# High parts of 32 attention-stage inputs: VectorE maximum over an axis of length one in place of a copy

## The chip, the cores and the metric

The kernel runs on one core of one Trainium2 chip. The metric is device microseconds (us) of one launch; the time before is the median of three runs. Engines are named as in the profile: PE is TensorE's matmul, PEld its weight load, DVE is VectorE, ACT ScalarE, POOL GpSimd, SP SyncE.

## The reference

One hybrid decoder layer in float32 on a sequence of 2048 rows of width 1024. Cut to what matters here:

```python
proj = h @ w_in[l]
x_rnn, z_rnn, q, k, v, z_attn, g_r, g_a = jnp.split(proj, IN_SPLITS, axis=-1)
...
y_rnn = (hr * jax.nn.silu(z_rnn)) @ w_out_rnn[l]             # RG-LRU branch, projected
...
o = dilated_attention_mixture(qh, kh, vh).reshape(B, S, D_ATTN)   # 8 heads of 128, three (window, dilation) groups
y_attn = (o * jax.nn.silu(z_attn)) @ w_out_attn[l]           # attention branch, projected
merged = jax.nn.sigmoid(g_r + bg_r) * y_rnn + jax.nn.sigmoid(g_a + bg_a) * y_attn
x = x + gate[:, None, :] * (merged @ w_o[l])
```

## The kernel before, in words

Every matmul operand is split into a high part, rounded to the PE's float32r type, and a low part, the difference; a product is three matmuls, high by high, high by low and low by high (`mm3`, line 152). So each operand costs one rounding copy and one subtraction on some engine. The helpers are `hi_act` (line 160, ScalarE), `hi_dve` (line 163, a VectorE copy, CAST in the profile), `lo_pool` (line 166, a GpSimd subtraction) and `lo_dve` (line 169, a VectorE subtraction).

The launch has three stages that follow one another: the input projection with the recurrence (to about 1340 us), attention (about 1340 to 1870 us), and the rest of the output projections with the last product.

Attention runs over 16 heads-and-halves of six units each. All engines follow one order written out by hand (`tc.manual_schedule`): each slot makes the scores of one unit (tiles `sc`), its exponentials (`pp`), and, seven slots later, the scaled and transposed weights (`pT`, split into `pth` and `ptl`) and the sums `o`. The transposes of line 1562 go to PSUM tiles `pT` that come free when the `ptl` subtraction has read them. GpSimd makes the low parts `kq`, `vh`, `wh` of the loaded keys, queries and values, and copies queries into window order (`q`, line 1436), which the window scores read. Once for each head-and-half, the softmax weights `M` are made by a chain of small VectorE instructions, lines 1648 to 1674, and ScalarE scales `pp` with them (line 1542).

The gaps between the attention matmuls are filled with steps of other work, the generator `steps(jobs)`: the two output projections, products `pj` of 128x128 weights `S` by 128x512 inputs `yh` and `yl`. There are eight jobs `j`, each of 512 columns; the first four read the recurrence's output, the last four the attention's. A job's eight inputs `k` are loaded into a ring of raw tiles `R` and split by `split_y`, in steps that the table `SPLIT_Y` fixes, around the start of the job. Jobs 1 to 4 have their high parts made by VectorE: 4 jobs of 8 inputs, 32 copies. Their low parts come from GpSimd for even `k` and from VectorE, right behind the copy, for odd `k`. The products are evicted at line 1786 into `fg`.

## Time and profile before

| What | Value |
|---|---|
| time, median of 3 runs | 2168.0 us (2166.8 to 2169.54) |
| the profiled execution's own time | 2169.62 us |
| its span, first to last instruction | 2167.8 us |
| mean granted TensorE clock | 0.998 |
| busy share of the span: PE, DVE, ACT, POOL | 99%, 69%, 60%, 51% |

The span is the profiler's, 1.8 us shorter than that execution's time; the profiled execution is 1.6 us above the median. Busy shares are means over the launch, and a busy PE includes matmuls that are pipelined behind one another.

### The profile page before, as it was taken

How to read it: one execution, taken by the hardware profiler on the slowest of the kernel's cores; microseconds unless marked ns; L12 is line 12 of the kernel's file. 1: busy time of each engine (PE TensorE's matmuls, PEld its weight loads, DVE VectorE, ACT ScalarE, POOL GpSimd, SP SyncE). 2: the span in 40 equal slices, each digit the busy share in tenths (PEclk: the TensorE clock that was granted, in tenths of full speed). 3: DMA queues.
4: the chain of work that ended last, by engine and by line, in shares of the span. 5: the costliest groups of instructions: out<-in, count | busy, mean ns of one | idle time of the engine just before them, and what ended most of it. 6: DMA issues, size and time to landing. Idle time of an engine off the chain costs nothing.

```text
span 2167.8 us, 32585 instructions
## 1 busy us (share of the span) xinstructions
PE 2138.3 (99%) x10539; PEld 1787.8 (82%) x10539; DVE 1488.1 (69%) x2606; ACT 1296.9 (60%) x2591; POOL 1111.2 (51%) x868
## 2 busy tenths in 40 slices
PE   9999999999999999999999999999999999999998
PEld 6888778888888888888888887888888988878886
DVE  6759878768656725544536584687777787788887
ACT  5748668668644527457548532677878877444333
POOL 1467667777666323223234564466666564422444
PEclk9999999999999999999999999999999999999999
DMA  8467887886655378898996666988887777899553
GB/s 302 144 208 259 277 290 264 285 296 237 175 112 165 108 250 281 295 312 299 323 327 220 163 163 198 288 266 266 269 267 230 242 241 223 298 316 295 183 171 111
DMA packets 416431, 521.39 MB, mean 241 GB/s; under 512 B 107558, under 2 KB 282882, under 8 KB 415236
## 3 DMA queue, kind: packets, MB, share of 16 engines
q1 hardware_dynamic: 376244, 401.65, 59.7%
q10 hardware_dynamic: 34384, 99.78, 12.1%
q0 software_dynamic: 5632, 17.88, 2.6%
q8 instruction: 83, 1.36, 0.3%
q14 instruction: 88, 0.72, 0.1%
HBM read 332.02 MB, written 187.17 MB: 240 GB/s over the span
## 4 chain that ended last, share of the span: by engine, by line
PE 63%; DVE 5%; DMA 5%; POOL 3%; issue 3%; ACT 1%; SPq 1%; POOLq 0%; ACTq 0%; DVEq 0%
PE X L152 13%; PE V L152 13%; PE pj L152 8%; PE Z L152 7%; PE W L152 6%; PE Y L152 6%; PE sc L152 3%; PE o L152 3%; PE pg L152 1%; DMA fg<-mrT 1%; PE pT L1562 1%; POOL kq L166 1%; PE pT L1575 1%; DMA fg<-gaT 1%; DMA oT<-zt 1%
## 5 line engine op out<-in xcount | busy, mean ns | idle before, releaser
L166 POOL TENSOR_TENSOR S<-R,S 128x512 fp32r<-128x512 f32 x192 | 294.3, 1541 | 170.0 <-ACT S L160 87.3
L152 PE MATMUL V<-T,S 128*128 128x512 f32 x1344 | 324.2, 390 | 2.3 <-DVE ev L455 2.3
L152 PE MATMUL X<-T,S 128*128 128x512 f32 x1344 | 323.8, 390 | 1.5 <-ACT u L385 1.3
L152 PE MATMUL pj<-yh,S 128*128 128x512 f32 x896 | 322.1, 403 | 1.3 <-DVE fg L1786 0.8
L152 PEld LDWEIGHTS V<-T,S 128*128 128x128 f32 x1344 | 251.8, 188 | 56.3 <-issue 2.1
L152 PEld LDWEIGHTS X<-T,S 128*128 128x128 f32 x1344 | 251.7, 188 | 56.4 <-ACT u L385 3.0
L166 POOL TENSOR_TENSOR S<-s,S 128x512 fp32r<-128x512 f32 x116 | 170.6, 1471 | 151.1 <-ACT S L160 114.9
L152 PEld LDWEIGHTS pj<-yh,S 128*128 128x128 f32 x896 | 168.5, 188 | 32.6 <-DVE S L169 1.6
L1475 ACT ACTIVATE pp<-pp,st 128x256 f32<-128x256 f32 (+3 forms) x256 | 133.7, 523 | 73.1 <-DVE st L1474 71.7
L152 PE MATMUL pj<-yl,S 128*128 128x512 f32 x448 | 175.9, 393 | 0.6 <-POOL yl L166 0.3
L160 ACT ACTIVATE S<-s 128x512 fp32r<-128x512 f32 x124 | 77.4, 624 | 145.4 <-DVE s L285 91.0
L152 PE MATMUL W<-T,S 128*128 128x512 f32 x672 | 161.6, 389 | 0.0
L152 PE MATMUL Y<-T,S 128*128 128x512 f32 x672 | 161.5, 389 | 0.0
L152 PE MATMUL Z<-T,S 128*128 128x512 f32 x672 | 161.4, 389 | 0.0
L160 ACT ACTIVATE S<-R 128x512 fp32r<-128x512 f32 x200 | 121.6, 623 | 59.0 <-DMA R<-in_w_in_dram 14.8
L169 DVE TENSOR_TENSOR ptl<-pT,pth 128x384 fp32r<-128x384 f32 (+1 forms) x160 | 97.9, 628 | 76.0 <-ACT pth L160 73.7
L152 PEld LDWEIGHTS W<-T,S 128*128 128x128 f32 x672 | 126.0, 188 | 26.9 <-issue 0.9
L152 PEld LDWEIGHTS Z<-T,S 128*128 128x128 f32 x672 | 126.1, 188 | 26.2
L152 PEld LDWEIGHTS Y<-T,S 128*128 128x128 f32 x672 | 126.1, 188 | 26.1
L974 DVE SCALAR_TENSOR_TENSOR xc<-xr,par,xc 128x512 f32<-128x512 f32 x96 | 104.4, 1087 | 58.1 <-ACT xc L968 55.9
L166 POOL TENSOR_TENSOR s<-R,s 128x512 fp32r<-128x512 f32 x32 | 43.2, 1351 | 189.5 <-ACT s L160 173.0
L1542 ACT ACTIVATE pp<-pp,M 128x256 f32<-128x256 f32 (+3 forms) x256 | 117.9, 522 | 22.3 <-DVE M L1674 22.3
(417 smaller groups left out, 4922.8 us busy)
## 6 DMA issues: line engine op xcount, KB each, us to landing
sD<-S ACTq DMA_DIRECT2D x140, 512.0 KB, 3.8
S<-sD SPq DMA_DIRECT2D x140, 512.0 KB, 5.2
S<-wD SPq DMA_DIRECT2D x82, 512.0 KB, 5.6
R<-in_w_in_dram SPq DMA_DIRECT2D x144, 256.0 KB, 3.4
wD<-s ACTq DMA_DIRECT2D x64, 256.0 KB, 5.3
kraw<-kqT SPq DMA_DIRECT2D x32, 384.0 KB, 5.4
T<-in_w_mod_dram SPq DMA_DIRECT2D x16, 512.0 KB, 9.1
vN<-ev SPq DMA_DIRECT2D x32, 256.0 KB, 2.7
```

Source lines behind the costliest of these rows:

```text
L152: nc.tensor.matmul(o, lhsT=l, rhs=r, start=st, stop=sp, **kw)
L160: nc.scalar.activation(o, i, AF.Copy)
L166: nc.gpsimd.tensor_tensor(o, i, h.bitcast(F32), ALU.subtract)
L169: return nc.vector.tensor_tensor(o, i, h.bitcast(F32), ALU.subtract).ins
L974: nc.vector.scalar_tensor_tensor(xc, xr[:, i : i + CH], cw(i), xc, ALU.mult, ALU.add)
L1475: nc.scalar.activation(pdst, pdst, AF.Exp, bias=m_, scale=-1.0, accum_out=l_)
L1542: nc.scalar.activation(pp, pp, AF.Copy, scale=w)
L1562: nc.tensor.transpose(pt[:, c0 + j * P : c0 + (j + 1) * P], pp[i][:, k * P : (k + 1) * P], ident)
L1575: nc.tensor.transpose(pt[:, c * P : (c + 1) * P], pp[:, half * P : (half + 1) * P], ident)
```

## The change

`split_y` no longer calls the copy for jobs 1 to 4. It has VectorE take the maximum over an added innermost axis of length one, with the same tile read and the same tile written; a maximum of one number is that number, rounded on writing as the copy's was. The order of the instructions, what each waits for and every other instruction are as before, on all engines: on VectorE 32 rows of CAST become rows of TENSOR_REDUCE in the same places.

```diff
-                (hi_dve if 0 < j < NB + 1 else hi_act)(yh[:], t[:])
+                if 0 < j < NB + 1:
+                    nc.vector.tensor_reduce(yh[:], t[:].unsqueeze(2), AX.X, ALU.max)
+                else:
+                    hi_act(yh[:], t[:])
                 (lo_dve if (k % 2 if j else k > 4) or j > NB + 1 else lo_pool)(yl[:], t[:], yh[:])
```

## The prediction

> **What bounds the kernel now.** I read the page's engine shares first, then the busy time by stretches of the attention stage, then the PE's waits in it, and last the instructions in order of time around those waits.

> ```profile
> PE 2138.3 (99%) x10539; PEld 1787.8 (82%) x10539; DVE 1488.1 (69%) x2606; ACT 1296.9 (60%) x2591; POOL 1111.2 (51%) x868
> ```

> The PE is the bound: only 2167.8 - 2138.3 = 29.5 us of the span lack a matmul. Next come the stretches of the stage that holds the 32 copies (start:end, length, then busy time of PE, PEld, DVE, ACT, POOL).

> ```profile
> 1380.00:1620.00 240.00, 239.30 (x1578) 214.17 (x1578) 184.88 (x567) 191.34 (x587) 153.35 (x145) 1.00 0.86 272
> 1620.00:1640.00 20.00, 16.10 (x100) 13.22 (x99) 17.64 (x46) 10.80 (x27) 13.98 (x12) 1.00 0.65 191
> 1640.00:1760.00 120.00, 120.00 (x796) 109.23 (x795) 90.06 (x244) 103.29 (x260) 76.02 (x60) 1.00 0.79 244
> 1760.00:1780.00 20.00, 17.78 (x109) 15.88 (x107) 17.42 (x42) 14.64 (x40) 13.91 (x13) 0.91 0.66 194
> ```

> From 1380 to 1780 us the PE lacks 0.70 + 3.90 + 0 + 2.22 = 6.8 us. Nearly all of it lies in two stretches of 20 us. That is the most a cheaper high part can give back, unless waits hide inside matmuls. Who ended the PE's waits from 1380 to 1880 us (total us, times, longest):

> ```profile
> PE sc L152 <- POOL q L1436: 4.6, 5, 1.7
> PE pT L1562 <- DVE ptl L169: 1.3, 2, 0.7
> PE pT L1562 <- ACT pp L1542: 1.0, 2, 0.7
> PE pj L152 <- POOL yl L166: 0.3, 1, 0.3
> ```

> **The change: 32 copies go, 32 maxima come.** The groups of this stage, the first with min/median/max in ns, the others with busy us and mean ns:

> ```profile
> L163 DVE CAST yh<-R x32: 409/423/2073, 1394.5 to 1768.5; 128x512 fp32r<-128x512 f32 x32
> ...
> L163 DVE CAST yh<-R 128x512 fp32r<-128x512 f32 x32 | 22.6, 710 | 0.0
> ...
> L169 DVE TENSOR_TENSOR yl<-R,yh 128x512 fp32r<-128x512 f32 x18 | 19.7, 1101 | 0.5
> ```

> A copy that nothing holds up takes 0.42 us; the mean is 0.71. So 22.6 - 32 x 0.423 = 9.1 us are waiting inside the copies. The rows below say for what: each long copy spans a GpSimd instruction and ends just behind it.

> The trace has no 128x512 maximum. The nearest rows are VectorE's other reductions, and the pass of 512 numbers at line 1474:

> ```profile
> L1653 DVE TENSOR_REDUCE xs<-xq x16: 285/286/287, 1378.8 to 1837.9; 128x32 f32<-128x128 f32 x16
> ...
> L1658 DVE TENSOR_REDUCE sc<-xq x16: 215/217/220, 1379.0 to 1838.1; 128x16 f32<-128x64 f32 x16
> ...
> L1474 DVE CUSTOM_DVE_ANT_0 pp<-sc,msk 128x512 f32<-128x512 f32 x32 | 22.0, 689 | 1.1
> ```

> By numbers read, the slope is (286 - 217) / 64 = 1.08 ns, and 512 numbers cost 286 + 384 x 1.08 = 700 ns. By numbers written it is 69 / 16 = 4.3 ns, and 512 results cost 286 + 480 x 4.3 = 2350 ns: both reductions fold four numbers into one, so these rows can't tell the two apart. The lower end is the free copy's 423 ns. I take 0.69 us, since line 1474, which writes as many numbers as it reads, lies there too; 0.42 and 2.35 stay for the range.

> Does a maximum wait for GpSimd? Here a reduction runs inside a GpSimd instruction that lasts to 1632.58, and its 16 durations above differ by 2 ns. Line 1672, a small addition of two SBUF tiles, does wait when GpSimd is at work: 1.20 us there, 0.17 elsewhere.

> ```profile
> 1630.74 1.84 POOL L166 TENSOR_TENSOR kq<-kraw,kq 128x768 fp32r<-128x768 f32 x1
> ...
> 1631.15 0.29 DVE L1653 TENSOR_REDUCE xs<-xq 128x32 f32<-128x128 f32 x1
> ...
> 1634.71 1.29 POOL L166 TENSOR_TENSOR yl<-R,yh 128x512 fp32r<-128x512 f32 x1 [0.36 <-DVE yh L163]
> ...
> 1634.83 1.20 DVE L1672 TENSOR_TENSOR M<-M,t__3081_16175 128x16 f32<-128x16 f32 x1
> ...
> L1672 DVE TENSOR_TENSOR M<-M,t__3271_17104 x1: 174/174/174, 1701.7 to 1701.7; 128x16 f32<-128x16 f32 x1
> ```

> So the maximum does not wait. VectorE's total: 32 x 0.69 = 22.1 us against 22.6, next to nothing; what changes is where the time lies. A free copy gets 0.27 us longer, a held one up to 1.4 us shorter.

> [...]

> **Place one, 1615 to 1634 us.** Rows of the timeline (start, us):

> ```profile
> 1615.78 2.69 DVE L163 CAST yh<-R 128x512 fp32r<-128x512 f32 x2
> ...
> 1615.80 1.04 PE L1575 MATMUL pT<-cs,pp 128*128 128x128 f32 x8
> ...
> 1616.15 4.03 POOL L166 TENSOR_TENSOR kq<-kraw,kq 128x768 fp32r<-128x768 f32 x2
> ...
> 1618.51 2.22 DVE L169 TENSOR_TENSOR yl<-R,yh 128x512 fp32r<-128x512 f32 x1
> ...
> 1620.65 0.68 DVE L163 CAST pth<-pT 128x512 fp32r<-128x512 f32 x1
> ...
> 1622.20 0.63 PE L1562 MATMUL pT<-cs,pp 128*128 128x128 f32 x4 [0.65 <-DVE ptl L169]
> ...
> 1624.48 0.62 ACT L1475 ACTIVATE pp<-pp,st 128x384 f32<-128x384 f32 x1 [4.61 <-DVE st L1474]
> ...
> 1628.77 0.62 ACT L160 ACTIVATE vh<-vraw 128x512 fp32r<-128x512 f32 x1
> ...
> 1629.47 1.30 POOL L166 TENSOR_TENSOR vh<-vraw,vh 128x512 fp32r<-128x512 f32 x1 [2.70 <-DMA vraw<-vN]
> ...
> 1632.53 1.82 POOL L1436 CAST q<-kq 128x512 fp32r<-128x512 f32 x2
> ...
> 1633.39 0.51 PE L152 MATMUL sc<-kq,q 128*128 128x256 f32 x2 [1.05 <-POOL q L1436]
> ```

> Two copies sit out GpSimd's first `kq`; the subtraction behind them misses the gap and sits out the second. With maxima, VectorE reaches the subtraction at 1615.8 + 2 x 0.69 = 1617.2, before the first `kq` ends (about 1618.2, half of 4.03 on). It gets in there and ends at about 1618.8 instead of 1620.7. So `pth`, whose input the PE had made by 1616.8, starts 1.8 us earlier, and both PE waits on `ptl`, 1.3 us, go. Behind it ScalarE, which waited 4.61 us for VectorE, comes up to 1.8 us earlier too. Its `vh`, which ended at 1629.39, released GpSimd's `vh` (the transfer named there I read as landed before). From 1627.7 on, 1.30 for `vh`, 1.84 for `kq` and some 0.6 for the first `q` make 1631.4, where the PE got it at 1633.4. The PE asks for it 1.3 us earlier, so its wait of 1.05 shrinks to about 0.4. Gain here: 1.3 + 0.7 = 2.0 us. The price: GpSimd's second `kq` starts 0.5 us later, which its idle time before `vh` covers.

> **Place two, 1760 to 1772 us.**

> ```profile
> 1760.42 1.30 POOL L166 TENSOR_TENSOR vh<-vraw,vh 128x512 fp32r<-128x512 f32 x1
> 1760.52 1.49 DVE L163 CAST yh<-R 128x512 fp32r<-128x512 f32 x1
> ...
> 1761.69 2.03 POOL L166 TENSOR_TENSOR kq<-kraw,kq 128x768 fp32r<-128x768 f32 x1
> ...
> 1762.05 2.22 DVE L169 TENSOR_TENSOR yl<-R,yh 128x512 fp32r<-128x512 f32 x1
> ...
> 1764.19 1.14 DVE L169 TENSOR_TENSOR ptl<-pT,pth 128x512 fp32r<-128x512 f32 x2
> ...
> 1765.26 0.41 DVE L163 CAST yh<-R 128x512 fp32r<-128x512 f32 x1
> ...
> 1765.74 1.30 POOL L166 TENSOR_TENSOR yl<-R,yh 128x512 fp32r<-128x512 f32 x1 [2.02 <-DMA vraw<-vN]
> ...
> 1770.89 0.50 PE L152 MATMUL sc<-kq,q 128*128 128x256 f32 x2 [1.71 <-POOL q L1436]
> ```

> The maximum ends at 1761.2, the subtraction gets in when `vh` ends (1761.72) and ends at 1762.3 instead of 1764.3. The second high part, behind the two `ptl`, then ends near 1762.4 + 1.14 + 0.69 = 1764.2 instead of 1765.7, and GpSimd's `yl`, which I read as waiting for it and not for the transfer named, starts about 1.4 us earlier; `vh`, `kq` and `q` follow it. The PE lost 1.71 and then 0.52 us on these `q`; I take 1.3 us back, since a `yl` subtraction now gets in ahead of the first `q`.

> **Costs.** A maximum ahead of the chain that makes `M` delays it by up to 0.27 us, and behind it the PE waits for `pp` (1.0 us at present). For such chains in the later two rings of copies, 2 x 0.2 = 0.4 us. The other free copies have VectorE idle time behind them: 240.0 - 184.9 = 55 us from 1380 to 1620, where the PE lacks 0.7.

> **Sum.** 2.0 + 1.3 - 0.4 = 2.9 us. The profiled execution goes from 2169.6 to 2166.7, and as it was 1.6 us above the median, the median goes from 2168.0 to 2165.1.

> **The rivals.**

> *The wait only moves.* The subtraction behind the odd maxima reads two tiles of SBUF and waited as the copies did: 18 of them took 1.10 us in the mean, against 0.69. If it meets a GpSimd instruction each time, VectorE is no earlier at either place, and the time stays at 2168, with 0.4 us of cost 2168.4. For it: the 2.22 us rows. Against: in both rows the copy's own wait is what made it miss the gap. [...] Chance 0.27.

> *More comes back.* All 6.8 us of the PE's idle time, or the like with waits hidden in matmuls: 2161.2. For it: both places start from the same late VectorE. Against: `q` waits for three GpSimd instructions that the change leaves alone. Chance 0.22.

> *The maximum is paid by result, 2.35 us.* Slower than before: VectorE would have 32 x (2.35 - 0.71) = 52 us more. In the densest stretch

> ```profile
> 1400.00:1420.00 20.00, 19.88 (x137) 17.97 (x136) 17.51 (x56) 14.49 (x50) 14.37 (x15) 1.00 0.88 258
> ```

> six of a ring's eight copies add 9.8 us to 2.5 idle ones; 7.3 us on the path, four times, gives 2197. It decides once a maximum costs more than 0.71 + 2.5 / 6 = 1.1 us. Against: line 1474 writes 512 numbers in 0.69. Chance 0.06.

> *The change doesn't do what it says*, as a copy after all: the instruction list has reductions in those 32 places, one for one; under 0.01.

> **How the numbers follow.** A measurement of this kernel tells about 0.2%, 4.3 us, from no change: below 2163.7 is faster, above 2172.3 slower. The forecast has 0.45 and covers 2163.5 to 2167; the moved wait 0.27 lies within 0.2%; the larger gain 0.22 lies mostly below 2163.7; the price by result 0.06 is slower. The forecast's lower edge adds a little to faster: 0.23, same 0.70, slower 0.07. The range takes in the large gain and the moved wait with the median's own scatter of 1.5 us: 2161.2 to 2169.5.

> **What would show it.** Right: maxima all near 0.69 us with a maximum close to the minimum; `yl` near 1618 and 1762 shorter than 2.22 us; no PE wait on `ptl`; less than 4.6 us on `q`. Wrong: maxima above 1.1 us or spread up to 2 us; or `yl` means well above 1.1 us and the PE's waits as before, in which case the wait has only moved.

## The result

Over 22 executions of each kernel on the same chip the changed kernel takes 2163.5 us (median), the kernel before 2167.16 us: ratio 0.9986, 95% interval 0.9980 to 0.9991, that is 2 to 4 us less, 3.0 at the ratio. One execution in the comparisons below, of `copies_k6`, took 2350 us at a mean granted clock of 0.85 and is left out of its ratio.

The groups of the changed lines in the attention stage (min/median/max in ns; then count, busy us and mean ns):

```profile
L1771 DVE TENSOR_REDUCE yh<-R x32: 669/677/683, 1393.1 to 1764.3; 128x512 fp32r<-128x512 f32 x32
...
L1771 DVE TENSOR_REDUCE yh<-R 128x512 fp32r<-128x512 f32 x32 | 21.5, 677 | 0.0
L169 DVE TENSOR_TENSOR yl<-R,yh 128x512 fp32r<-128x512 f32 x18 | 18.2, 1018 | 0.6
```

All 32 maxima take the same time to within 14 ns, where the copies took 409 to 2073 ns: none of them waited. VectorE's total for them hardly moves, 21.5 us against 22.6. The subtractions behind them still wait, a little less: mean 1018 ns against 1101, and one of them takes 2422 ns.

The stretches of the stage, as shown of before (start:end, length, busy PE, PEld, DVE, ACT, POOL, granted clock, DMA share, GB/s):

```profile
1380.00:1620.00 240.00, 238.90 (x1578) 214.28 (x1577) 184.91 (x567) 191.25 (x586) 154.42 (x147) 1.00 0.86 271
1620.00:1640.00 20.00, 18.02 (x117) 15.57 (x115) 16.31 (x46) 14.94 (x39) 13.98 (x12) 1.00 0.70 195
1640.00:1760.00 120.00, 120.00 (x800) 109.47 (x800) 91.85 (x240) 103.16 (x259) 77.19 (x59) 1.00 0.80 254
1760.00:1780.00 20.00, 17.94 (x108) 15.93 (x107) 17.20 (x44) 13.78 (x34) 13.75 (x12) 0.91 0.64 194
```

From 1620 to 1640 us the PE lacks 1.98 us in place of 3.90. From 1760 to 1780 it lacks 2.06 in place of 2.22: next to nothing came back there. Its waits from 1380 to 1880 us:

```profile
PE sc L152 <- POOL q L1436: 4.0, 4, 2.0
PE pj L152 <- POOL yl L166: 1.0, 2, 0.6
PE pT L1562 <- ACT pp L1542: 0.8, 2, 0.6
PE sc L152 <- ACT sm L1630: 0.3, 1, 0.3
```

The two waits on `ptl` are gone; the longest wait on `q` is as long as ever. The instructions in order of time at place one:

```profile
1614.16 1.27 DVE L1771 TENSOR_REDUCE yh<-R 128x512 fp32r<-128x512 f32 x2
1614.28 4.12 POOL L166 TENSOR_TENSOR kq<-kraw,kq 128x768 fp32r<-128x768 f32 x2
1615.47 1.22 DVE L169 TENSOR_TENSOR yl<-R,yh 128x512 fp32r<-128x512 f32 x1
1616.61 0.68 DVE L163 CAST pth<-pT 128x512 fp32r<-128x512 f32 x1
```

Two maxima run through GpSimd's first `kq`, the subtraction arrives before that one ends, waits 0.5 us, gets in between the two `kq` and takes 1.22 us where it took 2.22. From the start of the pair to `pth` it is 2.45 us; it was 4.87.

To see where the PE came forward, I took the start of the same weight load (all kernels here have the same 10539 in the same order) in each profile, less its start in the first profile of the kernel before. The table gives by how much this difference changes in each part of the stage, in us; a minus means that the PE came forward. Parts are by the time of the kernel before. A ring is the eight inputs of a job. Half clock means that the granted TensorE clock fell to 0.50 in that part.

| Profile | ring of job 1, 1380 to 1440 | job 2, 1440 to 1550 | job 3, 1550 to 1650 | 1650 to 1760 | job 4, 1760 to 1790 | half clock in 1760 to 1790 |
|---|---|---|---|---|---|---|
| before, first | 0 | 0 | 0 | 0 | 0 | yes |
| changed, first | +0.13 | -0.57 | -2.36 | 0 | -0.16 | yes |
| changed, second (after_again) | +0.12 | -0.58 | -2.36 | 0 | -1.70 | no |

At 1380 us, ahead of any changed instruction, the first profile of the changed kernel was 1.43 us in front already. That is chance, and no part of the change's 2.8 us up to 1650 (0.13 - 0.57 - 2.36).

The halved clock has to be equal on both sides of a comparison: a further profile of the kernel before, without it (before_look1), has -1.55 from 1760 to 1790 us, so that the changed kernel's -1.70 is 0.15 us of gain. Behind the table some is given back. From 1790 to 1880 us the three rows have 0, +0.30 and +0.55, and before_look1 -0.39; the PE now waits 0.3 to 0.5 us there for ScalarE (`sm`, line 1630), which it does not in the kernel before. Up to 1880 us the change therefore brings 2.7 us between the profiles with the halved clock and 2.1 us between those without.

### The profile page after: what moved, and what is told of

The parts are those of the page before. It is cut to its first block, busy times and chain, and to the rows that moved or that the text cites. A ratio compares the mean times of both kernels' runs of the same rounds, so it can differ in the third digit from the quotient of the medians.

```text
span 2163.4 us, 32584 instructions
## 1 busy us (share of the span) xinstructions
PE 2137.6 (99%) x10538; PEld 1788.5 (83%) x10539; DVE 1487.2 (69%) x2606; ACT 1296.6 (60%) x2591; POOL 1109.5 (51%) x868
## 3 DMA queue, kind: packets, MB, share of 16 engines
q1 hardware_dynamic: 376244, 401.65, 59.8%
## 4 chain that ended last, share of the span: by engine, by line
PE 68%; DVE 6%; DMA 3%; issue 2%; POOL 1%; ACT 1%; SPq 0%; POOLq 0%; ACTq 0%; DVEq 0%
PE X L152 13%; PE V L152 13%; PE pj L152 9%; PE Z L152 7%; PE W L152 7%; PE Y L152 6%; PE sc L152 4%; PE o L152 4%; PE pg L152 1%; DMA fg<-mrT 1%; PE pT L1562 1%; PE pT L1575 1%; DMA fg<-gaT 1%; DVE ptl L169 1%; DMA meT<-fg 1%
## 5 line engine op out<-in xcount | busy, mean ns | idle before, releaser
L166 POOL TENSOR_TENSOR S<-R,S 128x512 fp32r<-128x512 f32 x192 | 294.5, 1542 | 169.8 <-ACT S L160 82.6
L152 PE MATMUL V<-T,S 128*128 128x512 f32 x1344 | 324.3, 390 | 1.9 <-DVE ev L455 1.9
L152 PE MATMUL X<-T,S 128*128 128x512 f32 x1344 | 323.9, 390 | 1.5 <-ACT u L385 1.2
L152 PE MATMUL pj<-yh,S 128*128 128x512 f32 x896 | 321.9, 403 | 0.7 <-DVE S L169 0.6
L152 PEld LDWEIGHTS X<-T,S 128*128 128x128 f32 x1344 | 251.7, 188 | 56.5 <-ACT u L385 2.8
L152 PEld LDWEIGHTS V<-T,S 128*128 128x128 f32 x1344 | 251.9, 188 | 55.9 <-issue 1.7
L166 POOL TENSOR_TENSOR S<-s,S 128x512 fp32r<-128x512 f32 x116 | 170.7, 1472 | 150.5 <-ACT S L160 114.0
L152 PEld LDWEIGHTS pj<-yh,S 128*128 128x128 f32 x896 | 168.5, 188 | 32.0 <-DVE S L169 1.9
L152 PE MATMUL pj<-yl,S 128*128 128x512 f32 x448 | 176.0, 393 | 1.2 <-POOL yl L166 1.0
L1475 ACT ACTIVATE pp<-pp,st 128x256 f32<-128x256 f32 (+3 forms) x256 | 133.7, 523 | 71.3 <-DVE st L1474 70.3
L160 ACT ACTIVATE S<-s 128x512 fp32r<-128x512 f32 x124 | 77.3, 623 | 145.2 <-DVE s L285 88.2
L152 PE MATMUL W<-T,S 128*128 128x512 f32 x672 | 161.6, 389 | 0.0
L152 PE MATMUL Y<-T,S 128*128 128x512 f32 x672 | 161.5, 389 | 0.0
L152 PE MATMUL Z<-T,S 128*128 128x512 f32 x672 | 161.4, 389 | 0.0
L160 ACT ACTIVATE S<-R 128x512 fp32r<-128x512 f32 x200 | 121.5, 622 | 59.1 <-DMA R<-in_w_in_dram 15.0
L169 DVE TENSOR_TENSOR ptl<-pT,pth 128x384 fp32r<-128x384 f32 (+1 forms) x160 | 97.8, 628 | 74.3 <-ACT pth L160 72.1
L152 PEld LDWEIGHTS W<-T,S 128*128 128x128 f32 x672 | 126.0, 188 | 26.9 <-issue 0.9
L152 PEld LDWEIGHTS Z<-T,S 128*128 128x128 f32 x672 | 126.1, 188 | 26.2
L152 PEld LDWEIGHTS Y<-T,S 128*128 128x128 f32 x672 | 126.1, 188 | 26.2
L166 POOL TENSOR_TENSOR s<-R,s 128x512 fp32r<-128x512 f32 x32 | 43.4, 1357 | 187.2 <-ACT s L160 158.2
L1542 ACT ACTIVATE pp<-pp,M 128x256 f32<-128x256 f32 (+3 forms) x256 | 118.0, 523 | 21.0 <-DVE M L1674 21.0
```

The lines of the kernel that those rows point to most:

```text
L152: nc.tensor.matmul(o, lhsT=l, rhs=r, start=st, stop=sp, **kw)
L160: nc.scalar.activation(o, i, AF.Copy)
L166: nc.gpsimd.tensor_tensor(o, i, h.bitcast(F32), ALU.subtract)
L169: return nc.vector.tensor_tensor(o, i, h.bitcast(F32), ALU.subtract).ins
L1475: nc.scalar.activation(pdst, pdst, AF.Exp, bias=m_, scale=-1.0, accum_out=l_)
L1542: nc.scalar.activation(pp, pp, AF.Copy, scale=w)
```

## The experiments

**Which copies carry the gain.** Maximum in job 3 alone, and the complement.

```diff
-                if 0 < j < NB + 1:
+                if j == 3:                     # and, in the complement: j in (1, 2, 4)
                     nc.vector.tensor_reduce(yh[:], t[:].unsqueeze(2), AX.X, ALU.max)
+                elif 0 < j < NB + 1:
+                    hi_dve(yh[:], t[:])
```

> Maximum in job 3 alone (8 of 32), copies in jobs 1, 2 and 4. Theory (the gain comes from the one place near 1615 us, where two copies and the subtraction behind them sit out GpSimd one after the other): 2.3 us less than before, nearly the whole gain, with the PE pulling ahead between 1615 and 1640 us. Rival (each maximum brings its share, by less holding-up of either engine): a quarter of 3.7 us, 0.9 us less.

> The complement: maximum in jobs 1, 2 and 4 (24 of 32), copies in job 3. Theory: at most 0.6 us less than before, and the PE's two waits on ptl near 1622 us are there again. Rival (each its share): three quarters of 3.7 us, 2.8 us less.

Measured: ratio 0.9994 (0.9984 to 1.0005) and 0.9998 (0.9988 to 1.0007). The times alone settle nothing; executions of one kernel spread over up to 10 us on that chip. The profiles do, one of each kernel. The PE's waits from 1610 to 1650 us, maximum in job 3 alone:

```profile
PE sc L152 <- POOL q L1436: 1.1, 2, 0.6
PE pT L1562 <- ACT pp L1542: 0.8, 2, 0.6
```

and the complement:

```profile
PE sc L152 <- POOL q L1436: 1.6, 2, 1.1
PE pT L1562 <- DVE ptl L169: 1.3, 2, 0.7
PE pT L1562 <- ACT pp L1542: 1.0, 2, 0.7
```

By the parts of the table above, job 3 alone gives 0.00, +0.02, -2.34, 0, -0.01; the complement +0.15, -0.56, +0.02, 0, -0.12. So 8 of the 32 maxima bring 2.34 of 2.80 us, the other 24 bring 0.4, and the parts add up to the changed kernel's. The rival of equal shares is out.

**Is it the waiting, or the length?** The tile's maximum with itself, which reads two SBUF inputs.

```diff
-                    nc.vector.tensor_reduce(yh[:], t[:].unsqueeze(2), AX.X, ALU.max)
+                    nc.vector.tensor_tensor(yh[:], t[:], t[:], ALU.max)
```

> All 32 high parts as a maximum of the tile with itself, an instruction of two SBUF inputs: the same result and about the same 0.68 us when free, but held up by GpSimd as the copies are. Theory (it is the waiting for GpSimd that the change takes away): no gain; single durations up to 2 us as with the copies, the place near 1615 us as late as before; 2167 to 2170 us, 0 to 3 us more than before. [...]

Measured: 2177.51 us, ratio 1.0048 (1.0036 to 1.0060), 10.4 us more. Its groups, as above:

```profile
L1771 DVE TENSOR_TENSOR yh<-R x32: 675/690/2339, 1393.1 to 1776.7; 128x512 fp32r<-128x512 f32 x32
...
L1771 DVE TENSOR_TENSOR yh<-R 128x512 fp32r<-128x512 f32 x32 | 31.2, 981 | 0.0
```

Free it costs 0.69 us like the reduction, but it takes up to 2.34 us, 0.98 us in the mean. Every ring loses: +3.43, +1.86, +3.05 and +1.49 us; about 1.9 of the 3.05 come with a halved clock, which lasted 6.83 us near 1640 us. The same result at the same length loses 10 us with the wait and gains 3 without it: the waiting is what counts. It is mostly VectorE's: the maxima and the subtractions behind them take 52.2 us in the stage, in the changed kernel 39.7, and GpSimd's `kq` of 768 columns 61.2 against 59.8. My 0 to 3 us were too few: even ring 1, which the reductions leave within 0.13 us, loses 3.4. I had counted what one instruction is longer, not which gaps it then misses; those I did not follow one by one.

**What holds place two.** In the changed kernel:

```profile
1756.15 1.33 POOL L166 TENSOR_TENSOR vh<-vraw,vh 128x512 fp32r<-128x512 f32 x1
...
1756.69 0.68 DVE L1771 TENSOR_REDUCE yh<-R 128x512 fp32r<-128x512 f32 x1
...
1757.40 2.42 DVE L169 TENSOR_TENSOR yl<-R,yh 128x512 fp32r<-128x512 f32 x1
1757.40 1.87 POOL L166 TENSOR_TENSOR kq<-kraw,kq 128x768 fp32r<-128x768 f32 x1
...
1761.56 1.28 POOL L166 TENSOR_TENSOR yl<-R,yh 128x512 fp32r<-128x512 f32 x1 [2.28 <-DVE yh L1771]
...
1766.95 2.46 PE L152 MATMUL sc<-kq,q 128*128 128x256 f32 x9 [1.97 <-POOL q L1436]
```

The subtraction and GpSimd's `kq` start in the same hundredth of a us, and the subtraction loses: it sits out all of `kq`. It lacks some hundredths of a us. To bring it there 0.61 us earlier, one eviction ahead of it was set later:

```diff
-                if k == 1 and t:
+                if k == (4 if t == NB * KT else 1) and t:
                     evict(t - 1, last)
```

> The changed kernel with one eviction of a product (line 1786 of the kernel before) in job 4 set three steps later, so that VectorE reaches the maximum of input 5 and the subtraction behind it 0.61 us earlier, near 1757 us; nothing else is reordered. Theory (in the changed kernel that subtraction misses the end of GpSimd's vh by a few hundredths of a us and sits out the whole kq): the subtraction takes 1.2 to 1.4 us in place of 2.42, GpSimd's next low part starts 0.8 us earlier, the PE's pause before q falls from 2.0 us to 0.7 to 1.2; 0.8 us less than the changed kernel, and 2.5 us less if the halved clock goes with it. Rival (it is not a matter of that moment): the subtraction takes 2.4 us as before and the time is the changed kernel's.

Measured: 2162.17 us, ratio 0.9980 (0.9972 to 0.9989), beside 0.9988 (0.9979 to 0.9996) for the changed kernel in the same comparison; these intervals overlap, so the profiles have to tell the two apart. In the same place of the program:

```profile
1756.04 1.30 POOL L166 TENSOR_TENSOR vh<-vraw,vh 128x512 fp32r<-128x512 f32 x1
1756.69 1.19 DVE L169 TENSOR_TENSOR yl<-R,yh 128x512 fp32r<-128x512 f32 x1
1757.28 2.31 POOL L166 TENSOR_TENSOR kq<-kraw,kq 128x768 fp32r<-128x768 f32 x1
...
1765.68 2.06 PE L152 MATMUL sc<-kq,q 128*128 128x256 f32 x12 [0.87 <-POOL q L1436]
```

The subtraction takes 1.19 us, `kq` follows it, and the PE's pause falls from 1.97 to 0.87 us. The part from 1760 to 1790 us is 1.15 us shorter than in profiles of the changed kernel without the halved clock (-2.85 against -1.70), 2.7 us shorter than in those with it. That it was a matter of that moment is shown. The loss behind 1790 us stays (+0.62).

**Taking GpSimd's wait out of the chain.** The changed kernel, with one low part moved:

```diff
-                (lo_dve if (k % 2 if j else k > 4) or j > NB + 1 else lo_pool)(yl[:], t[:], yh[:])
+                (lo_dve if (k % 2 if j else k > 4) or j > NB + 1 or (j, k) == (NB, 6) else lo_pool)(yl[:], t[:], yh[:])
```

> The changed kernel with one more edit: the low part of input 6 of job 4 goes from GpSimd to VectorE. In the changed kernel GpSimd waits 2.28 us for that input's high part near 1761 us with vh, kq and q queued behind it, and the PE then waits 1.97 us for q, after which its granted clock is 0.50 for some 3.4 us. Theory (the pause and the halved clock both hang on this queue): the wait goes and with it the halved clock, 2.0 + 1.7 = 3.7 us less than the changed kernel, 7 us less than before. Rival 1 (the wait on q stays, for VectorE's 0.69 us more delays what GpSimd needs): same as the changed kernel. Rival 2 (the halved clock does not come from that pause): 2.0 us less than the changed kernel.

Measured: 2160.98 us, ratio 0.9974 (0.9963 to 0.9984): 6 us less than before, the lowest median here, though its interval overlaps that of the moved eviction, which ran on another chip. From 1760 to 1790 us the PE's only waits are now

```profile
PE pT L1562 <- ACT pp L1542: 1.1, 2, 0.8
```

The wait on `q` is gone, no halved clock follows, and 1.1 us go to a wait further on, which I had not counted: this part is 2.2 us shorter than in the changed kernel's first profile (-2.40 against -0.16), not 3.7. Of these 2.2 us 1.5 are the halved clock: against the changed kernel's profiles without it, 0.7 us are left (-2.40 against -1.70). From 1790 to 1880 us another 0.7 to 1.0 us come back (-0.40 against +0.30 and +0.55). That one profile has no halved clock does not show by itself that the pause causes it, since the changed kernel has profiles without it too; the last section has more. The same edit on the kernel before (copies):

> The kernel before (copies in all four jobs) with only the low part of input 6 of job 4 moved from GpSimd to VectorE. Theory (the two edits act at two places, the maxima near 1615 us, this one near 1765 us): the PE's 2.2 us of waits on q near 1770 us and the halved clock behind them go, the waits on ptl near 1622 us stay; 2163.5, 3.6 us less than before. Rival (the edit needs the maxima, since with copies VectorE is 1.9 us late at that place and sits out a GpSimd instruction before it can make the low part): 1 us less than before or nothing.

Measured: ratio 0.9995 (0.9986 to 1.0004); the part from 1760 to 1790 us is 1.13 us shorter than in the first profile of the kernel before, the others up to there unchanged. But that profile had the halved clock and this one has not: against before_look1, without it, the part is 0.42 us longer (-1.13 against -1.55). The edit without the maxima gains nothing there but the clock. The rival had it: with copies VectorE is late, and the moved subtraction itself took 2.19 us there, against 0.93 with maxima. And with input 6 moved in all four jobs (the condition `k == 6 and 0 < j` moves that of job 5 as well, behind 1860 us, beyond the parts given):

> The changed kernel with the low part of input 6 moved from GpSimd to VectorE in all of jobs 1 to 4, not in job 4 alone. Theory: as with job 4 alone, 2161; in job 1 the PE's 0.6 us wait on a GpSimd low part near 1421 us goes, in job 3 VectorE has 0.69 us more ahead of the softmax weights that the PE waits for: between 1 us less and 0.5 us more than with job 4 alone. Rival (every low part off GpSimd brings the same 2.5 us): 2154.

Measured: 2162.97 us, ratio 0.9987 (0.9978 to 0.9996). Parts: +0.63, +0.11, -2.64, +0.10, -2.40. Jobs 1 and 2 lose 1.1 us against the edit in job 4 alone, job 3 wins 0.3. Moving low parts off GpSimd is no good in itself; my half a us at worst was too little.

**The changed kernel again, and further profiles of both.**

> The changed kernel itself once more, beside the others. If the missed gap near 1757 us and the gain near 1615 us are fixed by the order of events, the profile shows both again: subtraction of 2.42 us, a PE wait of 2.0 us on q, half clock behind it, no PE wait on ptl; time 3.7 us less than before. If they are chance, one of them differs.

> The kernel before, one more profile. Theory (the PE's pause near 1770 us only sometimes is followed by a halved clock, by chance of the moment): the pause of 2.2 us is there in all profiles, the halved clock in some, and the stretch from 1760 to 1790 us is 1.6 us shorter where it is missing. Rival (the pause's length decides): the same pause, the same halved clock each time. The waits on ptl near 1622 us are there in either case.

> As the first further profile of the kernel before: pause of 2.2 us near 1770 us, waits on ptl near 1622 us; halved clock by chance (theory) or always (rival).

> The changed kernel, one more profile: pause of 2.0 us on q near 1765 us in all profiles, halved clock by chance (theory) or always (rival; the second profile of this kernel, which had the pause without it, already speaks against). No waits on ptl near 1620 us; the stretch from 1612 to 1650 us 2.4 us shorter than in each profile of the kernel before.

> As the first further profile of the changed kernel: pause of 2.0 us on q, halved clock by chance (theory) or always (rival), no waits on ptl.

The stretch from 1760 to 1790 us (columns as above; the granted clock is the last but two) in the first profile of the changed kernel, then the second:

```profile
1760.00:1790.00 30.00, 27.94 (x173) 24.91 (x172) 23.72 (x62) 22.40 (x57) 17.14 (x15) 0.94 0.74 234
```

```profile
1760.00:1790.00 30.00, 27.93 (x185) 25.14 (x184) 24.57 (x64) 23.38 (x59) 19.33 (x15) 1.00 0.76 242
```

The same 2 us of pause, a clock of 0.94 in the one and of 1.00 in the other, and 1.54 us between them. Over all profiles, the changed kernel had the halved clock here in 2 of 4, the kernel before in 2 of 3; the waits on `q` were there in all. The parts repeat closely: from 1550 to 1650 us the four profiles of the changed kernel give -2.36, -2.36, -2.36 and -2.33, the two further ones of the kernel before +0.01 and +0.15.

## Why the prediction was right

- **The price of the maximum.** 0.69 us taken, 0.677 measured, no wait: right. The estimates by numbers read (0.70 us) and from line 1474 (0.69 us) held; the price by result (2.35 us) is out.
- **Place one.** 2.0 us forecast, 2.36 measured for its part. The subtraction did what the rows said, the waits on `ptl` went, and the wait on `q` fell from 1.05 to 0.6 us (0.4 forecast). The `ptl` side was worth more than its 1.3 us of waits: from 1618 to 1626 us the PE comes forward 1.73 us, and the rest brings 0.6 of the 0.7 us forecast.
- **Place two.** 1.3 us forecast, 0.1 to 0.2 measured, and more than that given back behind 1790 us. The sign set for it, a `yl` near 1762 shorter than 2.22 us, failed with 2.42. The step that failed is "the subtraction gets in when `vh` ends": I left GpSimd where it was. But `vh` starts 0.54 us ahead of the maximum now, where it was 0.10 ahead of the copy. Part of that can be read in the pair of `kq` ahead of it, before and then after the change:

```profile
1755.35 3.86 POOL L166 TENSOR_TENSOR kq<-kraw,kq 128x768 fp32r<-128x768 f32 x2
```

```profile
1751.26 3.69 POOL L166 TENSOR_TENSOR kq<-kraw,kq 128x768 fp32r<-128x768 f32 x2
```

  It takes 0.17 us less, with no copy beside it; the other 0.27 us of the shift arise ahead of this pair. So here the rival of the moved wait was right, at the one place where it mattered by hundredths.
- **Costs.** The 0.4 us for the softmax weights did not come: those waits went from 1.0 to 0.8 us. Another 0.13 us did: near 1421 us the PE now waits 0.6 us for a GpSimd low part, and most of it comes back near 1433 us.
- **Not forecast:** 0.57 us in the ring of job 2. The complement shows it too, so it is the maxima there. The traces place 0.46 us of it near 1516 us, at the PE's weight loads for the transposes, which wait 0.7 us for `pp` in the kernel before and 0.2 in the changed one. Ahead of that a copy of 0.95 us and a subtraction of 1.12 us beside GpSimd become 0.68 and 0.69, and VectorE comes 0.7 us sooner to the chain that makes `M`. It is the mechanism of place one at a place where the row of PE waits shows none.

The sum, 2.9 us, was met (2.8 up to 1650 us, 3.0 at the ratio of the times) because place one and job 2 gave about what place two withheld. The forecast of the total was better than its parts, by luck. The median came out at 2163.5 and not at 2165.1: 0.8 us of that is the kernel before, whose median over 22 executions is 2167.2 and not 2168.0, and the rest over the parts is within the ratio's interval and the spread of the runs.

## What to carry to other kernels

Look at an instruction's spread, not at its median: a copy that takes 0.42 us free and 2.07 at worst may be worse than one that always takes 0.68, if a queue with work of its own stands behind it. Follow the wait to the next instruction on the same engine that was also held up (here the subtraction, 0.68 us free and 2.42 at worst), and ask whether it now meets a gap or just misses it; when both engines move, read the margin in the new order of events and not in the old. A forecast with two places and one of them within 0.5 us of a gap deserves a range that has both outcomes.

## What the runs showed of the hardware that I had not expected

After a PE pause of about 2 us (1.97 to 2.2 us on `q`) the granted clock was 0.50 for 3.41 us in some executions and stayed at 1.00 in others of the same kernel: it fell in 4 of the 7 profiles of the two kernels, at a price of 1.1 to 1.6 us in that part. That is 0.94 over 30 us in the rows above. The profiles of `job3_only`, `jobs_124` and `two_input_max`, which kept such a pause, had it too. With the longest wait there down to 1.0 us or less, none of the profiles of the four kernels with an edit there showed it. In the first profile of the changed kernel the wait of 1.97 us and the 1.54 us of the halved clock behind it make 3.5 us.

The traces show what went ahead of the falls in this stage. In each of the nine profiles in which the clock fell more than once, the starts of the falls lie whole multiples of 3.4133 us apart (389.12 us, 114 times, in the first profile of the kernel before; 392.53 us, 115 times, in the first of the changed one; 1860.26 us, 545 times, in before_look1). These starts fit a grid of stretches of that length, and every profile has a fall at its very end from which it can be counted back. At place two, the stretch just ahead of a fall holds 1.56 to 2.42 us without a matmul, in all seven profiles with a fall. In the three that had the pause and no fall, the pause lies across a boundary, and the fullest stretch holds 1.43 to 1.52 us. The stretch ahead of the fall in the first profile of the changed kernel, the one in after_look2, and the fullest in after_again, without a fall (columns as above, length less busy PE is the time without a matmul):

```profile
1764.15:1767.56 3.41, 1.35 (x11) 1.00 (x9) 3.31 (x8) 1.10 (x3) 3.35 (x3) 1.00 0.66 193
```

```profile
1768.57:1771.98 3.41, 1.85 (x13) 1.65 (x14) 3.31 (x8) 0.88 (x3) 2.01 (x3) 1.00 0.90 285
```

```profile
1765.04:1768.46 3.42, 1.90 (x13) 1.69 (x14) 3.32 (x8) 0.89 (x2) 1.98 (x3) 1.00 0.88 287
```

Whether a kernel without the pause varies less is open. The seven runs with the one low part moved lie within 2.3 us, the 25 of the kernel before beside them within 10; but the eleven of the changed kernel's second comparison, pause and all, lie within 2.3 us too, and before_look1, before_look2, after_look2 and `k6_all` had a fall near 300 us besides.
